# Loading the last rows of a convolution's input as f16 by GpSimd, in pieces of 5, 120 and 3 partitions

## The chip, the cores and the metric

The kernel runs on one core of a Trainium2 chip. The metric is the device time of one execution in microseconds (us). The kernel before takes 128.01 us (median; its first runs lay between 127.67 and 128.04). A profile accompanies the runs; its times count from the start of the profiled span, which is 1.8 us shorter than the device time. Sixteen DMA engines move all data between memory and the core. They are the subject of this document.

## The reference, cut to what matters

```python
batch, c_in, h, w, c_out, k, dilation = 16, 64, 64, 64, 128, 3, 2
x_pad = np.pad(x, ((0, 0), (0, 0), (pad, pad), (pad, pad)), mode='constant')
# for every image b, output channel co, input channel ci, and 3 x 3 taps kh, kw:
output[b, co] += weight[co, ci, kh, kw] * x_pad[b, ci, kh*dilation:kh*dilation+h, kw*dilation:kw*dilation+w]
```

Input is 16.8 MB and output 33.6 MB, both f32. That is what the DMA engines have to carry, whatever the arithmetic does.

## The kernel before: the parts that matter

Two images of 64 channels fill the 128 partitions; such a pair is loaded as f32, cast to f16 by ScalarE in four chunks of rows, multiplied by TensorE, summed by VectorE into an f32 output tile, and stored. There are eight pairs, and four groups of 16 output rows in each.

```python
    def load(pb, cuts=(0, H), queue=nc.sync):
        x32_tiles[pb] = fpool.tile([P, HW], f32, tag="x32", name="x32")
        for lo, hi in zip(cuts[:-1], cuts[1:]):
            queue.dma_start(
                out=x32_tiles[pb][:, lo * W : hi * W], in_=x_pair[pb, :, lo * W : hi * W]
            )
    # ... (cast(c) copies one chunk of rows, f32 to f16, on ScalarE)
    def casts(G):
        for n in range(2 if G else 3):
            c = ahead[0]
            if c >= ngroups or c > G + (7 if c < 2 * NG else 3):
                return
            cast(c)
            ahead[0] += 1
            if c % NG == NG - 1 and c // NG + XF < npairs:
                k = c // NG + XF
                load(k, (0, H) if k == XF else (0, H // 2, H), queue=nc.scalar)
    # ... (the loop over the 32 groups: products, copy of psP, two adds, then)
        if pb in (0, npairs - 1):
            if g % 2 == 1:
                store(pb, 0, (g - 1) * GR, (g + 1) * GR)
                store(pb, 1, (g - 1) * GR, (g + 1) * GR)
        elif g == NG - 1:
            store(pb, 0)
            store(pb, 1)
```

## Time and profile before

| | kernel before |
|---|---|
| time, median | 128.01 us |
| end of the last VectorE add | 109.9 us |
| end of the span | 126.2 us |
| last store: first, second last, last completion count | 121.46, 123.22, 125.23 us |

The view of windows gives, for stretches of the span, the busy time of each engine, TensorE's granted clock, the mean busy share of the 16 DMA engines and what they moved. The kernel before:

```profile
core 0: us, PE busy (x) PEld busy (x) DVE busy (x) ACT busy (x) POOL busy (x), PEclk, DMA share, GB/s
12.00:60.00 48.00, 47.56 (x462) 26.25 (x463) 42.54 (x47) 30.04 (x32) 0.00 (x0) 1.00 1.01 418
75.00:90.00 15.00, 15.00 (x148) 8.24 (x146) 13.18 (x15) 9.89 (x10) 0.00 (x0) 1.00 1.02 432
112.00:120.00 8.00, 0.00 (x0) 0.00 (x0) 0.00 (x0) 0.00 (x0) 0.00 (x0) 0.50 1.00 421
120.00:127.00 7.00, 0.00 (x0) 0.00 (x0) 0.00 (x0) 0.00 (x0) 0.00 (x0) 0.50 0.32 135
```

TensorE looks full until 108 us, but so do the DMA engines, and from 112 us on DMA works alone, at full rate. The SyncE queue's waits, in us in total, times, and longest, agree: the end of the kernel is a wait for stores.

```profile
SPq L279 <- DMA out_dram<-osb: 13.7, 1, 13.7
```

Two more lines of the page, the ScalarE casts and the DMA queues (packets, MB, share of the 16 engines' span):

```profile
L73 ACT CAST x<-x 128x1024 f16<-128x1024 f32 (+2 forms) x31 | 32.1, 1044 | 0.3 <-DMA x<-in_x_dram 0.3
...
q1 hardware_dynamic: 3600, 40.14, 75.5%
q10 hardware_dynamic: 1296, 10.49, 20.3%
```

One thing is not on the page. Each transfer has a semaphore which every DMA engine raises by one when its share has landed, and the trace records the time of each raise. For the last store of the kernel before, in us:

```
121.46 121.47 121.71 121.82 122.22 122.25 122.29 122.88 122.91 123.04 123.12 123.14 123.14 123.14 123.22 125.23
```

Fifteen engines finish within 1.8 us, and one comes 2.0 us after all others. I call these sixteen times the completion counts. The span ends 1.0 us after the last of them.

### The profile page before, as it was taken

How to read it: one execution, taken by the hardware profiler on the slowest of the kernel's cores; microseconds unless marked ns; L12 is line 12 of the kernel's file. 1: busy time of each engine (PE TensorE's matmuls, PEld its weight loads, DVE VectorE, ACT ScalarE, POOL GpSimd, SP SyncE). 2: the span in 40 equal slices, each digit the busy share in tenths (PEclk: the TensorE clock that was granted, in tenths of full speed). 3: DMA queues.
4: the chain of work that ended last, by engine and by line, in shares of the span. 5: the costliest groups of instructions: out<-in, count | busy, mean ns of one | idle time of the engine just before them, and what ended most of it. 6: DMA issues, size and time to landing. Idle time of an engine off the chain costs nothing.

```text
span 126.2 us, 2341 instructions
## 1 busy us (share of the span) xinstructions
PE 104.9 (83%) x1000; PEld 56.7 (45%) x1000; DVE 90.7 (72%) x103; ACT 65.0 (51%) x68; POOL 2.3 (2%) x8
## 2 busy tenths in 40 slices
PE   6984999999999999999999999999999999300000
PEld 2341555555555555555555555555556555100000
DVE  0650997988898888988979898889888887700000
ACT  4377794366656665666576666666666633000000
POOL 2400000000000000000000000000000000000000
PEclk9999999999999999999999999999999999955555
DMA  4999999899999999999999999999999999999960
GB/s 138 377 456 426 431 426 382 330 431 423 421 421 449 426 431 426 431 421 431 421 434 421 434 426 428 431 426 423 441 431 421 431 415 446 415 413 431 423 293 13
DMA packets 4906, 50.78 MB, mean 402 GB/s; under 512 B 544, under 2 KB 544, under 8 KB 800
## 3 DMA queue, kind: packets, MB, share of 16 engines
q1 hardware_dynamic: 3600, 40.14, 75.5%
q10 hardware_dynamic: 1296, 10.49, 20.3%
q8 instruction: 8, 0.13, 0.4%
q14 instruction: 2, 0.02, 0.0%
HBM read 17.07 MB, written 33.55 MB: 401 GB/s over the span
## 4 chain that ended last, share of the span: by engine, by line
PE 75%; DMA 6%; ACT 2%; issue 1%; DVE 1%; DVEq 1%; SPq 1%; ACTq 0%
PE psA L174 30%; PE psB L174 29%; PE psP L174 16%; DMA x<-in_x_dram 6%; DVE osb L233 1%; DVEq L279 1%; ACT p_sb L226 1%; ACT x L73 1%; SPq L64 0%; ACTq L64 0%; SPq L88 0%; DVEq L233 0%
## 5 line engine op out<-in xcount | busy, mean ns | idle before, releaser
L174 PEld LDWEIGHTS <-w_sb 64*128 64x128 f16 x960 | 54.6, 94 | 46.9 <-issue 2.1
L226 ACT COPY p_sb<-psP 128x1024 f32<-128x1024 f32 x32 | 32.4, 1012 | 37.5 <-PE psP L174 19.1
L233 DVE TENSOR_TENSOR osb<-psA,p_sb 128x1024 f32<-128x1024 f32 x32 | 39.2, 1224 | 14.3 <-PE psA L174 7.7
L174 PE MATMUL psA<-x,w_sb 64*128 64x496 f16 (+3 forms) x384 | 45.1, 365 | 0.5 <-ACT x L146 0.5
L174 PE MATMUL psB<-x,w_sb 64*128 64x496 f16 (+3 forms) x384 | 45.1, 365 | 0.0
L233 DVE TENSOR_TENSOR osb<-psB,p_sb 128x1024 f32<-128x1024 f32 x32 | 39.0, 1220 | 0.0
L73 ACT CAST x<-x 128x1024 f16<-128x1024 f32 (+2 forms) x31 | 32.1, 1044 | 0.3 <-DMA x<-in_x_dram 0.3
L174 PE MATMUL psP<-xs,w_sb 64*128 64x496 f16 (+1 forms) x192 | 26.0, 371 | 1.8 <-ACT p_sb L226 1.8
L85 DVE TENSOR_TENSOR xs<-x 128x512 f16<-128x512 f16 x32 | 13.3, 416 | 0.7 <-ACT x L73 0.7
L101 PE MATMUL dm<-zero 128*128 128x512 f16 x10 | 4.4, 561 | 1.2 <-DVE zero L93 1.2
L101 PEld LDWEIGHTS <-zero 128*128 128x128 f16 x10 | 1.1, 124 | 2.6 <-issue 1.3
L111 DVE CAST wd<-w 128x192 f16<-128x192 f32 x1 | 0.5, 505 | 2.4 <-DMA w<-in_weight_dram 2.4
L124 PEld LDWEIGHTS <-wd 128*64 128x64 f16 x30 | 1.0, 118 | 1.9 <-DVE wd L111 1.1
L124 PE MATMUL wt<-ident,wd 128*64 128x128 f16 x30 | 1.6, 241 | 0.2 <-DVE wd L111 0.2
L113 ACT ACT_TABLE_LOAD x1 | 1.3, 1283 | 0.7 <-PEq L265 0.7
L136 ACT CAST w_sb<-wt 128x384 f16<-128x384 f32 x1 | 0.5, 478 | 1.7 <-PE wt L124 1.7
L113 ACT CAST wd<-w 128x192 f16<-128x192 f32 x1 | 0.5, 538 | 1.5 <-DMA w<-in_weight_dram 1.5
L138 DVE CAST w_sb<-wt 128x384 f16<-128x384 f32 x1 | 0.6, 557 | 0.7 <-PE wt L124 0.7
L146 ACT CAST x<-x 128x512 f16<-128x512 f32 x1 | 0.6, 618 | 0.5 <-DMA x<-in_x_dram 0.5
L93 DVE MEMSET zero<- 128x256 uint32 x1 | 0.3, 272 | 0.9 <-PEq L265 0.9
L112 POOL TENSOR_TENSOR wd<-w 128x192 f16<-128x192 f32 x1 | 0.8, 807 | 2.3 <-DMA w<-in_weight_dram 2.3
L115 POOL CAST wd<-w 128x192 f16<-128x192 f32 x1 | 0.8, 803 | 0.0
(11 smaller groups left out, 3.8 us busy)
## 6 DMA issues: line engine op xcount, KB each, us to landing
out_dram<-osb SPq DMA_DIRECT2D x12, 2048.0 KB, 17.4
out_dram<-osb SPq DMA_DIRECT2D x8, 1024.0 KB, 14.6
x<-in_x_dram ACTq DMA_DIRECT2D x8, 1024.0 KB, 17.0
x<-in_x_dram SPq DMA_DIRECT2D x2, 2048.0 KB, 16.5
x<-in_x_dram ACTq DMA_DIRECT2D x1, 2048.0 KB, 15.3
x<-in_x_dram SPq DMA_DIRECT2D x1, 1088.0 KB, 5.6
x<-in_x_dram SPq DMA_DIRECT2D x1, 960.0 KB, 7.4
w<-in_weight_dram SPq DMA_DIRECT2D x1, 288.0 KB, 2.8
```

Source lines behind the costliest of these rows:

```text
L73: nc.scalar.copy(out=x16_tiles[pb][:, lo * W : hi * W], in_=x32_tiles[pb][:, lo * W : hi * W])
L85: nc.vector.tensor_tensor(out=s, in0=v[:, :, 0], in1=v[:, :, 1], op=add)
L101: nc.tensor.matmul(out=dm[:, 0:512], lhsT=zero[:, 0:P], rhs=zero)
L112: nc.gpsimd.tensor_tensor(out=wdv[:, 3], in0=wv[:, 0], in1=wv[:, 1], op=sub)
L113: nc.scalar.copy(out=wdv[:, 2], in_=wv[:, 0])
L115: nc.gpsimd.tensor_copy(out=wdv[:, 4], in_=wv[:, 2])
L124: nc.tensor.matmul(out=wts[k % 3][r * CI : (r + 1) * CI, c0 + j * CO : c0 + (j + 1) * CO], lhsT=wd[:, t * CI : (t + 1) * CI], rhs=ident,)
L138: nc.vector.tensor_copy(out=t2[0], in_=t2[1])
L174: nc.tensor.matmul(out=po, lhsT=w_sb[pp, t * CO : (t + 1) * CO], rhs=rhs, start=first and j == 1, stop=last and j == 2,)
L226: nc.scalar.copy(out=p_sb, in_=psP)
L233: nc.vector.tensor_tensor(out=o[:, :, b0 : b0 + NBLK, e], in0=ps.rearrange("p (m b q) -> p m b q", m=2, q=2 * W), in1=pv, op=add,)
L279: with _tile.TileContext(nc) as tc:
```

## The change

For the last pair, rows 34 to 63 are no longer loaded as f32 and cast. GpSimd's DMA queue, which can convert during the transfer, writes them as f16 into the tile that the products read. The 128 partitions go in pieces of 5, 120 and 3. A fourth, tiny load into `turned` is read by nobody.

```diff
+    def load_cast(pb, r0):
+        lo = 0
+        for n in (5, 120, 3):
+            nc.gpsimd.dma_start(
+                out=x16_tiles[pb][lo : lo + n, r0 * W :], in_=x_pair[pb, lo : lo + n, r0 * W :]
+            )
+            lo += n
+        nc.gpsimd.dma_start(out=turned[0:9], in_=x_pair[pb, 0:9, 0:16])
@@ cast
         if g == 0:
             x16_tiles[pb] = xpool.tile([P, HW], f16, tag="x16", name="x16")
+            if pb == npairs - 1:
+                load_cast(pb, 2 * GR + d)
@@ casts
-            cast(c)
+            if c < ngroups - 2:
+                cast(c)
             ahead[0] += 1
             if c % NG == NG - 1 and c // NG + XF < npairs:
                 k = c // NG + XF
-                load(k, (0, H) if k == XF else (0, H // 2, H), queue=nc.scalar)
+                cuts = (0, H // 2, H) if k > XF else (0, H)
+                load(k, cuts if k < npairs - 1 else (0, GR, 2 * GR + d), queue=nc.scalar)
```

The odd pieces only make sense as an attempt to spare one DMA engine. If a round-robin cursor (a pointer that remembers which engine comes next) hands one engine to each row of a small piece and fifteen engines to the 120 rows, then 5 + 15 + 3 + 9 is 32, two full turns of 16, and the tiny load is there to bring the cursor back to its start.

More of the change, by code (lines that the diff above doesn't have):

```diff
@@ L66, in load @@
             )
+    turned = wpool.tile([P, 16], f16, name="turned")
+    def load_cast(pb, r0):
[6 more added lines that the diff above has]
+        nc.gpsimd.dma_start(out=turned[0:9], in_=x_pair[pb, 0:9, 0:16])
     def cast(c):
```

## The prediction

> **What bounds the kernel.** Transfers. In the view of windows, 12 to 100 us has PE 87.6 of 88 us busy, but also DMA share 1.01 at 423 GB/s; after 108 us the engines are done (last matmul about 108.8, last VectorE add 109.9) while DMA runs on at 416 to 426 GB/s until about 120. SyncE's waits end with 13.7 us for the last stores. So the end is set by bytes: 50.78 MB over 16 DMA engines. And not evenly: in the trace's semaphore record, the last store's sixteen completion counts come at 121.46 to 123.22 us, and the last one at 125.23. One DMA engine is 2.0 us behind the next and 2.3 behind the median. The six stores before it show the same 2.0 us. That engine alone sets the end; the span closes 1.0 us after it.
>
> **What the change does.** It removes two casts of ScalarE (1.05 and 0.94 us) and adds four GpSimd issues. ScalarE is busy 51% and is not on the path: its relief is worth 0. The source bytes are the same (128 rows of 7,680 B, 291 ns per packet before); only the SBUF side halves, 0.49 MB.
> What counts is which engine carries which row. Before, each engine carried 8 rows of that piece. The Trainium skill ("DMA: Bandwidth & Descriptors", "Why a DMA increments its semaphore by 16 and not by 1") says that a transfer uses the largest k up to 16 that divides its partitions, and that a GpSimd transfer with k under 16 takes k consecutive engines from a round-robin cursor. So 5 rows go to five engines, 120 rows to the next fifteen (8 each), 3 rows to three starting at the engine left out; the tiny fourth load moves the cursor 9 more, 32 in all, back to its start. One engine then carries 2 rows instead of 8, six carry 9, nine carry 8. No trace shows this yet.
>
> **Cost.** If the light engine is the late one, it saves 6 x 291 ns = 1.75 us: its last count falls from 125.23 to about 123.5. The others may rise by one row, 123.22 + 0.29 = 123.5: balanced. Gain about 1.7 us, time about 126.3. If a cast packet costs by its f16 side (half, an estimate), the late engine saves 2.0 us. If the light engine is another, there is nothing to gain (0 to +0.3). I take the rotation of the cursor as aimed at the late engine, at 3 in 4.
>
> **Side effects.** The transfers wait for the third buffer of f16 x (pair 4's last product, about 73 us) and are needed at the row sum near 103: 30 us of room. They lie inside a saturated stretch, so total DMA work is conserved.
>
> **Prediction:** 126.4 us (-1.3%), range 125.6 to 128.1. Faster by over 2%: 0.07; within 2%: 0.90; slower: 0.03.
>
> **What would show it.** The last store's last count comes within 0.5 us of the second last, where it was 2.0; the second last stays within 0.4 us of 123.2; packets of the new queue take about 290 ns; PE still ends near 108.8; ScalarE busy falls by 2.0 us.
>
> **What would make it wrong.** The light engine is not the late one (gap stays 2.0, or grows by 0.3); cast packets run well over 291 ns; the late engine's delay comes back after 80 us; GpSimd's transfers add set-up at the start or end.

## The result, and the profile after

The changed kernel takes 128.49 us (median of four, 128.35 to 128.52). The ratio to the kernel before is 1.0041, with a 95% interval of 1.0023 to 1.0059. All ratios here are the mean time of one kernel's fast runs over that of the other's of the same rounds, so they are not quite the ratio of the medians that are quoted. The change made the kernel no faster (a loss of 0.4%), and the time is outside the predicted range by 0.4 us.

The same views after the change: windows, the wait at the end, the ScalarE casts, the queues, and GpSimd's issues (start, duration).

```profile
12.00:60.00 48.00, 46.89 (x454) 25.53 (x452) 41.16 (x46) 30.48 (x31) 0.00 (x0) 1.00 1.01 412
75.00:90.00 15.00, 15.00 (x148) 8.18 (x146) 13.29 (x15) 9.30 (x11) 0.56 (x2) 1.00 1.02 386
112.00:120.00 8.00, 0.00 (x0) 0.00 (x0) 0.00 (x0) 0.00 (x0) 0.00 (x0) 0.56 0.99 420
120.00:127.00 7.00, 0.00 (x0) 0.00 (x0) 0.00 (x0) 0.00 (x0) 0.00 (x0) 0.50 0.47 200
```

```profile
SPq L294 <- DMA out_dram<-osb: 12.5, 1, 12.5
```

```profile
L86 ACT CAST x<-x 128x1024 f16<-128x1024 f32 (+2 forms) x29 | 30.1, 1048 | 0.4 <-DMA x<-in_x_dram 0.4
...
q1 hardware_dynamic: 3600, 40.14, 75.9%
q10 hardware_dynamic: 1296, 9.50, 18.7%
q0 software_dynamic: 240, 0.49, 2.0%
```

```profile
73.34 1.72 POOL L73 DMA_DIRECT2D x<-in_x_dram  x3 [67.99 <-DVE osb L248]
75.04 0.52 POOL L77 DMA_DIRECT2D turned<-in_x_dram  x1
```

The casts fell by two and 2.0 us of ScalarE, and GpSimd issued its four transfers at 73.3 us, both as predicted. In the window from 75 to 90 us the rate seems lower, 386 instead of 432 GB/s. Of these 46 GB/s, 33 are bookkeeping: the record counts the 0.49 MB written as f16, no longer the 0.98 MB read (0.49 MB over 15 us). The wait at the end is 1.2 us shorter, but it began 1.3 us later.

The last store's completion counts after the change:

```
121.65 122.28 122.73 122.98 123.10 123.56 123.60 123.70 123.95 124.06 124.28 124.54 124.90 124.97 125.22 125.29
```

This looked to me like a success of the prediction, cancelled by something else: the gap of the last count is 0.07 us instead of 2.0, but all the others had come later; their mean rose from 122.69 to 123.80 us, with the last included. So the first theory, A or B below, was that the spared engine was the right one and that a common loss of 1.1 us ate the gain. Two things pointed to an early cause. TensorE's full clock is first recorded at 10.5 us in this profile and at 5.1 us in that of before. And by 70 us, before GpSimd did anything, the engines had moved 0.34 MB less (28.09 against 28.43 MB, summed from the packets), because some store packets between 41 and 61 us took up to 1.26 us instead of 0.61.

The clock shows in the timeline of one dummy matmul, first before, then after (start, duration in us):

```profile
5.79 0.39 PE L101 MATMUL dm<-zero 128*128 128x512 f16 x1
```

```profile
6.52 0.61 PE L114 MATMUL dm<-zero 128*128 128x512 f16 x1
```

### The profile page after: what moved, and what is told of

Read it like the earlier page. It is cut to its first block, busy times and chain, and to the rows that moved or that the text cites. A ratio compares the mean times of both kernels' runs of the same rounds, so it can differ in the third digit from the quotient of the medians.

```text
span 126.6 us, 2348 instructions
## 1 busy us (share of the span) xinstructions
PE 107.2 (85%) x1000; PEld 56.9 (45%) x1000; DVE 90.5 (72%) x103; ACT 63.2 (50%) x66; POOL 4.5 (4%) x12
## 4 chain that ended last, share of the span: by engine, by line
PE 82%; DMA 2%; DVE 1%; DVEq 1%; ACT 1%; issue 0%
PE psA L189 32%; PE psB L189 30%; PE psP L189 16%; DMA w<-in_weight_dram 2%; PE wt L137 2%; PE dm L114 2%; DVE osb L248 1%; DVEq L294 1%; ACT p_sb L241 1%; DVE wd L124 0%; DVEq L248 0%
## 5 line engine op out<-in xcount | busy, mean ns | idle before, releaser
L189 PE MATMUL psA<-x,w_sb 64*128 64x496 f16 (+3 forms) x384 | 46.1, 371 | 0.0
L86 ACT CAST x<-x 128x1024 f16<-128x1024 f32 (+2 forms) x29 | 30.1, 1048 | 0.4 <-DMA x<-in_x_dram 0.4
L114 PE MATMUL dm<-zero 128*128 128x512 f16 x10 | 5.0, 623 | 1.2 <-DVE zero L106 1.2
L73 POOL DMA_DIRECT2D x<-in_x_dram x3 | 1.7, 578 | 68.0 <-DVE osb L248 68.0
L137 PEld LDWEIGHTS <-wd 128*64 128x64 f16 x30 | 1.5, 162 | 2.6 <-DVE wd L124 1.3
L137 PE MATMUL wt<-ident,wd 128*64 128x128 f16 x30 | 2.2, 314 | 0.4 <-DVE wd L124 0.4
```

The costliest lines, as they stand in the source:

```text
L73: nc.gpsimd.dma_start(out=x16_tiles[pb][lo : lo + n, r0 * W :], in_=x_pair[pb, lo : lo + n, r0 * W :])
L86: nc.scalar.copy(out=x16_tiles[pb][:, lo * W : hi * W], in_=x32_tiles[pb][:, lo * W : hi * W])
L114: nc.tensor.matmul(out=dm[:, 0:512], lhsT=zero[:, 0:P], rhs=zero)
L137: nc.tensor.matmul(out=wts[k % 3][r * CI : (r + 1) * CI, c0 + j * CO : c0 + (j + 1) * CO], lhsT=wd[:, t * CI : (t + 1) * CI], rhs=ident,)
L189: nc.tensor.matmul(out=po, lhsT=w_sb[pp, t * CO : (t + 1) * CO], rhs=rhs, start=first and j == 1, stop=last and j == 2,)
```

## The experiments

Each kernel ran beside the kernel before on the same chip. There were eighteen runs after the first; e8 repeats the changed kernel, and e17 repeats e1. All gave correct results. The medians are of all executions of a run, the ratios of its fast ones alone (one execution of e4 and one of e17 were slow).

| run | GpSimd's pieces | median us | ratio (95%) |
|---|---|---|---|
| changed kernel | 5, 120, 3, tiny 9 | 128.49 | 1.0041 (1.0023 to 1.0059) |
| e8_after_again | the same | 128.49 | 1.0032 (0.9980 to 1.0085) |
| e1_even | 128 | 127.80 | 0.9977 (0.9949 to 1.0006) |
| e17_even_again | 128 | 128.38 | 1.0032 (1.0011 to 1.0052) |
| e7_four_even | 4 x 32 | 128.08 | 0.9978 (0.9933 to 1.0024) |
| e2_rot8 | tiny 8, 5, 120, 3, tiny 9, tiny 8 | 128.39 | 1.0035 (0.9991 to 1.0078) |
| e3_after_warm | 5, 120, 3, tiny 9 | 128.93 | 1.0063 (1.0024 to 1.0101) |
| e4_before_warm | none | 127.99 | 0.9991 (0.9963 to 1.0018) |
| e9_first4 | 4, 120, 4, tiny 9 | 128.20 | 1.0020 (1.0003 to 1.0037) |
| e10_first3 | 3, 120, 5, tiny 9 | 128.41 | 1.0037 (1.0015 to 1.0060) |
| e11_first2 | 2, 120, 6, tiny 9 | 128.34 | 1.0025 (1.0009 to 1.0042) |
| e18_120_8 | 120, 8 | 128.40 | 1.0046 (1.0029 to 1.0064) |
| e13_low4 | 96, 8 x 4 | 127.81 | 0.9982 (0.9948 to 1.0015) |
| e16_low5 | 88, 8 x 5 | 129.27 | 1.0092 (1.0056 to 1.0128) |

The five runs with tagged engines (e5, e6, e12, e14, e15) had one execution each and are told below.

### First call: is it the f16 path, the early clock, or the choice of the engine?

**e1_even**, one transfer over all partitions:

```diff
-        for n in (5, 120, 3):
-            nc.gpsimd.dma_start(... lo : lo + n ...)
-        nc.gpsimd.dma_start(out=turned[0:9], ...)
+        nc.gpsimd.dma_start(out=x16_tiles[pb][:, r0 * W :], in_=x_pair[pb, :, r0 * W :])
```

> The same f16 load by GpSimd, but in one transfer over all 128 partitions, so that nothing is moved between the DMA engines. Theory A (the redistribution works, and took the late engine back by about 1.5 us; a loss that is common to all engines cancels it, from the f16 path through GpSimd): the last engine stays about 2 us or more behind the second last, the median count of the last store stays near 123.8, and the time is 129.5 to 130.5 us. Theory B (the common loss is not of the f16 path but of this execution's early part, the late clock or collisions of stores): median count near 122.9, last engine about 2 us later, time 127.7 to 128.3. Theory C (the redistribution itself did nothing or harm): time at or below the changed kernel's 128.5, with the gap closed all the same.

**e2_rot8**, a tiny load of 8 rows ahead, and one of 8 behind:

```diff
+        nc.gpsimd.dma_start(out=turned2[0:8], in_=x_pair[pb, 0:8, 0:16])
         lo = 0
         for n in (5, 120, 3):
 ...
+        nc.gpsimd.dma_start(out=turned3[0:8], in_=x_pair[pb, 0:8, 0:16])
```

> The changed kernel with one tiny load of 8 rows ahead of the three pieces (and 8 more rows after, so that the cursor comes back): the engine that is spared is the one 8 places further. Theory A: the late engine is a fixed one and is not spared now, so the gap of the last store's last count is 2.0 to 2.6 us instead of 0.07, and the time is 1.3 to 2 us over the changed kernel, 129.8 to 130.5 us. Rival (no fixed late engine; the gap closed by chance or by the interleaving): gap under 1 us and time within 0.4 us of 128.5.

**e3_after_warm** and **e4_before_warm**, the changed kernel and the kernel before with one dummy matmul more:

```diff
-    dummies(6)
+    dummies(7)
```

> The changed kernel with seven instead of six dummy matmuls ahead of the weights, so that TensorE has no idle gap there. In the changed kernel's trace the full clock came at 10.5 us, in the kernel before at 5.1 us, and every store was issued 1.27 us later. Theory B (that delay shifts the stores against the loads and costs the common 1.1 us): full clock near 5 us, median count of the last store near 122.7 to 122.9, time 126.6 to 127.3. Theory A (the f16 path costs it): the clock may come early, the stores are issued 1 us earlier, the time stays 128.2 to 128.7.

> The kernel before with the same seventh dummy. Theory B: it had the early clock already in its profile, so within 0.3 us of the kernel before (127.7 to 128.2), and its spread over the rounds no larger. Theory A: the same. If it is over 0.5 us faster, the early clock is itself a matter of chance in the kernel before too.

The single f16 transfer took 127.80 us, so theory A's 129.5 fell. Its profiled execution was the slowest of its five (129.01 us; the others 127.70 to 127.97), so I do not read that profile for the time. The clock came at 6.6 us in the profile of e3_after_warm and its time was no better, 128.93 us: theory B's gain in time did not come. What B said of the counts does fit the traces. Full clock came after 10 us in two profiles only, the first of the changed kernel (10.5) and that of e1_even (10.2), and their last stores have median counts of 123.82 and 123.56 us. In the seventeen other profiles that are not slow it came by 6.6 us, and the median is 122.77 to 123.19, in that of e3_after_warm 122.97, where the last count was still 125.79. So the common lateness goes with the late clock and not with the pieces, though two profiles are an observation and no test, and without it the late engine is late again. Of e4_before_warm the profiled run was a slow one; its fast runs equal the kernel before. The Trainium skill ("TensorE: Matmul & The Clock Gate", "Part 1: The HAM clock gate (the "warmup" mystery)") says that the window that decides when the full clock comes runs freely and that the moment differs from run to run of the same kernel. The traces here agree: 10.5 us in the first profile of the changed kernel, 5.7 us in its second.

The rotation by 8 places changed nothing in the time, 128.39 us. Its profile had the late engine back, 1.80 us behind the second last (125.49 against 123.69). I took that as nearly what theory A expected of the gap (2.0 to 2.6), but the time it expected, 129.8, did not come.

### Second call: which engine is late?

Names for engines come from a trick. Four tiny loads of 4, 5, 8 and 12 rows follow the last store on the same queue. By the Trainium skill ("DMA: Bandwidth & Descriptors", "Why a DMA increments its semaphore by 16 and not by 1"), a transfer issued by SyncE uses the largest number of engines up to 16 that divides its rows, and takes the lowest-numbered ones. Each tiny load then waits its turn behind the store on exactly those engines. What the runs themselves show is the nesting: the load of 5 has the counts of the load of 4, each 0.17 to 0.19 us later, and one more.

```diff
+    for k in (4, 5, 8, 12):
+        nc.sync.dma_start(out=tags[k][0:k], in_=x_pair[0, 0:k, 0:16])
```

> The kernel before with four tiny loads of 4, 5, 8 and 12 rows behind its last store on the same queue. They move next to no bytes; each takes its place behind the store in the queues of the DMA engines that it uses, so its completion counts say when those engines finish. If such a load takes the lowest-numbered engines, the load of 5 holds one count more than the load of 4, that of engine 4, and the brackets 0 to 3, 4, 5 to 7, 8 to 11 and 12 to 15 can be told apart. Theory D (the spared engine is not the late one, which is a fixed one): the late count, some 2 us behind the others, is in no bracket or not in that of engine 4. The prediction's premise (the late engine is the one that the cursor spares, number 4 if the cursor starts at 0): the late count is in the loads of 5, 8 and 12 and not in that of 4. Theory E (no fixed late engine): another bracket than in the next run.

> The same four tiny loads behind the changed kernel. Theory D: the late count is in the same bracket as in the kernel before, and the spared engine, 1.7 us earlier than it would be, is the earliest count; if the cursor starts at 0 that earliest count is in the load of 5 and not in that of 4. Theory E: the late count is in another bracket than before.

**e7_four_even**: `for n in (32, 32, 32, 32)` and no tiny load.

> The f16 load by GpSimd in four transfers of 32 rows, 2 rows for every engine in each: four transfers, no redistribution. Theory D (the changed kernel pays for the ninth row on the late engine, 0.30 us, and not for the number of transfers): within 0.2 us of the single f16 transfer, about 127.8, and 0.4 to 0.7 us under the changed kernel of the same call. Rival F (what costs is that four transfers are set up, with sixteen completion counts each): within 0.2 us of the changed kernel.

**e8_after_again**: no edit.

> The changed kernel once more, on the same chip as the run of four even transfers. Theory D: 128.3 to 128.8, its profile with a last count 1.5 to 2.8 us behind the mean and a first count 1 us or more ahead of the mean. The prediction's reading of the first profile after (the late engine was taken back, the gap is 0.07 us): the gap stays under 0.5 us in this execution too.

The counts of the loads in e5_tag_before, where the last store ended at 123.95 and then 125.21 us:

```
load of 4: 121.72 121.82 122.17 122.39
load of 5: 121.89 122.00 122.34 122.58 125.39
```

The late count is in the load of 5 and not in that of 4: engine 4 is the late one in the kernel before. The prediction's aim at engine 4 was right. In e6_tag_after:

```
load of 4: 122.40 122.48 122.76 122.78
load of 5: 122.58 122.66 122.94 122.96 125.61
```

Engine 4 is as late after the change as before. It was not the one that was spared. (A second engine, between 8 and 11, was nearly as late in that execution.) The last store's first count, 120.57 us, is 1.1 us ahead of the next, so some engine was spared. I misread which: I took the 121.92 us that opens the load of 8 for that engine, and the load of 8 begins after engine 4, so I concluded 5, 6 or 7. But each tiny load comes after the store, and by a fraction of a microsecond: 120.57 has no partner in any of the four loads. The spared engine lies above 11.

The changed kernel again, e8_after_again, took 128.49 us. Its counts are what a second profile is for:

```
120.75 122.27 122.32 122.39 122.46 122.64 122.67 122.98 123.12 123.14 123.16 123.18 123.26 123.64 123.72 125.14
```

The late engine is 1.42 us behind the second last, and the spared one 1.5 us ahead of the second. The closed gap of the first profile was an accident of that execution, in which the other engines had been delayed.

Of the four even transfers, e7_four_even, theory D expected 0.4 to 0.7 us less than the changed kernel of the same call, and rival F about the same. The medians are 0.41 us apart (128.08 and 128.49), but the intervals overlap widely, so the times of this call decide nothing.

### Third call: move the spared engine

`for n in (5, 120, 3)` became (4, 120, 4), (3, 120, 5) and (2, 120, 6); e12_tag_after2 is the changed kernel with tiny loads of 5, 6, 7 and 16 rows.

> The changed kernel with pieces of 4, 120 and 4 rows: the spared engine moves one place down. The last runs showed that engine 4 is the late one, before and after the change, and that the spared engine of 5, 120, 3 is number 5, 6 or 7. Theory G (the mechanism of the prediction is right, only the cursor does not start at 0 but at 1, 2 or 3): one of the three kernels with 4, 3 and 2 rows in the first piece spares engine 4; its last store's last count falls from about 125.4 to about 123.6, no count is then over 1 us behind the second last, and its time is 126.6 to 127.2 us; the other two stay at 128.2 to 128.6. This one is it if the cursor starts at 1. Rival H (the late engine is fed by something that grows when it has room, or the rest of the kernel is the limit then): none of the three is under 127.5 us.

> Pieces of 3, 120 and 5 rows: the spared engine moves two places down. Theory G: this one spares engine 4 if the cursor starts at 2, then 126.6 to 127.2 us and a gap under 1 us; otherwise 128.2 to 128.6 us and a gap of about 2 us. Rival H: not under 127.5 us in any case.

> Pieces of 2, 120 and 6 rows: the spared engine moves three places down. Theory G: this one spares engine 4 if the cursor starts at 3, then 126.6 to 127.2 us and a gap under 1 us; otherwise 128.2 to 128.6 us and a gap of about 2 us. Rival H: not under 127.5 us in any case.

> The changed kernel with tiny loads of 5, 6, 7 and 16 rows behind its last store, to tell which of the engines 5, 6 and 7 is spared. Theory G: the earliest count, 1 us or more ahead of the next, is in the load of 6 and not in that of 5 if it is engine 5 (then the kernel with 4 rows first is the fast one), in that of 7 and not that of 6 if engine 6 (then 3 rows first), in neither if engine 7 (then 2 rows first). If the spared engine is not the same as there, the cursor's start differs between executions or chips.

None was fast: 128.20, 128.41 and 128.34 us, each with an early count near 120.4 to 121.0 and a late one 1.5 us behind the second last. In e12_tag_after2 the earliest count, 120.50, has its partner only in the load of 16 (120.67). If a cursor that starts at 1, 2 or 3 chose the engines, one of these kernels would have spared engine 4. None did: theory G, as it was put, fell. Which engine was spared in the three was not asked, so they do not rule out a cursor that starts elsewhere; the fourth call does.

What replaced it began from a line of the first profile after the change. Queue q0 of the changed kernel has 240 packets: 128 rows, 9 rows of the tiny load, and 103 packets of 4 bytes. Sixteen completion counts for each of four transfers make 64. The other 39 fit if every transfer is filled up to the same number of packets on all 16 engines: 16 - 5 = 11, 8 x 16 - 120 = 8, 16 - 3 = 13 and 16 - 9 = 7. The other kernels' q0 lines fit as well (e1_even, e7_four_even, e2_rot8, in this order):

```profile
q0 software_dynamic: 144, 0.49, 1.9%
```

```profile
q0 software_dynamic: 192, 0.49, 1.9%
```

```profile
q0 software_dynamic: 304, 0.49, 2.0%
```

Those are 128 + 16; 128 + 4 x 16; and 128 + 9 + 8 + 8 rows with 6 x 16 counts and 39 + 16 fillers. These lines show the filling, but not at which engine a transfer starts: a cursor would give the same counts for these pieces. Theory I adds that: every GpSimd transfer of n rows is laid out over all 16 engines from engine 0 upward, n/16 rows each, rounded up. The 120 rows give 8 to engines 0 to 14 and none to engine 15. The 5 and 3 rows add to the lowest engines. By it the change gave engine 15 none, engines 0 to 2 ten rows, 3 and 4 nine, and the late engine 4 one row more than before.

### Fourth call: the dose on engine 4

```diff
-        for n in (5, 120, 3):
+        for n in (96,) + 8 * (4,):    # e13_low4 (no tiny load)
+        for n in (88,) + 8 * (5,):    # e16_low5 (no tiny load)
```

e14_low4_tag is e13_low4 with tiny loads of 4, 5, 8 and 16 rows; e15_tag_after3 the changed kernel with tiny loads of 13, 14, 15 and 16.

> The f16 load in one piece of 96 rows and eight pieces of 4 rows. Theory I (no cursor: every GpSimd transfer of n rows starts at engine 0 and gives each engine n/16 rows, rounded up, in order, so 120 rows leave out engine 15 and nothing else, and 5 and 3 rows add to engines 0 to 4): engines 0 to 3 carry 6 + 8 = 14 rows, engine 4 and all above 6 instead of 8. The late engine 4 gains 2 x 304 ns = 0.6 us, less some 0.1 us for nine transfers; engines 0 to 3 finish near 124 and stay behind it. Last count about 124.7, time 127.4 to 127.8, against 128.0 for the kernel before. Theory G (a cursor that moves by 4 with each piece of 4): the eight pieces spread evenly, 8 rows each, time as the four even transfers, 127.9 to 128.2.

> The f16 load in one piece of 88 rows and eight pieces of 5 rows. Theory I: engine 4 belongs to the five that each small piece uses and carries 6 + 8 = 14 rows, 6 more than in an even load, 1.82 us: last count near 127, time 129.4 to 130.2 us, 2 us or more above the kernel with pieces of 4. Theory G (cursor): 40 rows over 16 engines, 2 or 3 each, beside 8 from the large piece at most: within 0.5 us of the kernel with pieces of 4.

> The kernel with pieces of 4 rows, with tiny loads of 4, 5, 8 and 16 rows behind its last store. Theory I: the load of 4 holds four counts near 123.5 to 124.3, later than in the kernel before (121.7 to 122.4); the load of 5 adds that of engine 4, still the last of all, at 124.7 to 125.2 instead of 125.4 to 125.6. Theory G: the four counts stay at 121.7 to 122.8.

> The changed kernel with tiny loads of 13, 14, 15 and 16 rows behind its last store. Theory I: the earliest count, 1 us or more ahead of the next, is in the load of 16 alone, so it is engine 15. Theory G: it is in the load of 13, 14 or 15 too.

In e15_tag_after3 the earliest count of the last store is 120.36 us. The loads of 15 and of 16 begin:

```
load of 15: 122.36 122.67 122.83
load of 16: 120.53 122.53 122.88
```

The early engine is in the load of 16 alone: the change spared engine 15.

By theory I the two kernels differ in this: with pieces of 5 and 88 rows, engine 4 carries 14 rows instead of 6, and engines 14 and 15 carry 4 and none instead of 6 each. The other engines carry the same. They took 127.81 and 129.27 us on the same chip: 1.46 us apart. A cursor would have given every engine 8 rows in the first, and none over 11 in the second (88 rows on eleven engines, 8 each, and the small pieces 2 or 3), so at 0.304 us a row an estimate of 0.9 us apart at most. In e14_low4_tag engines 0 to 3 had become late instead (123.70, 123.82, 124.04 and 125.04 us in the load of 4, against 121.72 to 122.39 in the kernel before, on another chip), and the count that the load of 5 adds, engine 4, is 124.89 us, down from 125.39. That all four lowest engines became late by 1.9 us and more is what eight pieces starting at engine 0 do; a cursor would have spread them. (I had expected engine 4 to be still the last of all; one of engines 0 to 3 was, at 125.04.) The filler rule fits too, 128 + 9 x 16 counts + 96 fillers in both (8 x 12 with pieces of 4; 8 + 8 x 11 with pieces of 5). Here it does decide something: 88 rows on eleven engines of 8 rows would have to be filled up by 40 and not by 8. The q0 lines of e13_low4 and of e16_low5:

```profile
q0 software_dynamic: 368, 0.49, 2.0%
```

```profile
q0 software_dynamic: 368, 0.49, 2.0%
```

As many packets, the same bytes, other engines, 1.46 us. The sizes were off: I had expected 129.4 us or more and a difference of 2 us or more. Between 6 and 14 rows the time moved by 0.18 us a row (1.46 us over 8), not by the packet's 0.30, and engine 4's own count in the traces by as little (124.70 in the last store of e14_low4_tag; 126.12, the last count, in e16_low5: 1.42 us). Its lateness is not simply the sum of its packets, and why not stays open.

### Fifth call: what does the 0.4 us consist of?

e17_even_again is e1_even once more; e18_120_8 has pieces of 120 and 8.

> The single f16 transfer over 128 partitions again, on the same chip as the next run. Theory I: engine 4 carries 8 rows as in the kernel before, so within 0.3 us of the kernel before, 127.7 to 128.1; the f16 path itself costs nothing that shows.

> Pieces of 120 and 8 rows and nothing else: engines 0 to 7 carry 9 rows, 8 to 14 carry 8, engine 15 none. Theory I: engine 4 has one row more than in the single transfer, 0.30 us, and one more transfer: 128.1 to 128.4 us, 0.3 to 0.5 us over the single transfer, its first count 1 us or more ahead of the second (engine 15) and its last count again about 2 us behind. Rival F (the loss of the changed kernel is that of four transfers and the small one): within 0.1 us of the single transfer.

The times did not settle it. The single transfer took 128.38 us here and 127.80 in the first call, on another chip; its two intervals do not overlap, so they do not cover what differs between calls. The pieces of 120 and 8 took 128.40, not apart from the single transfer of the same call. The spared engine was there once more (first count 120.09, second 121.88).

## Why the prediction was wrong

- **What bounds the kernel: right.** DMA runs at 421 GB/s from 112 to 120 us with all other engines done, and the last count of the last store sets the end. In e16_low5 and e13_low4 as many packets on other engines moved the time by 1.46 us.
- **ScalarE's relief is worth nothing: right.** 2.0 us less of casts, no gain.
- **Cast packets cost what f32 packets cost: right.** They took 304 ns, against 291 before. The half cost that the prediction held possible did not show.
- **The late engine is one fixed engine and the change is aimed at it: half right.** It is engine 4 in the runs that named it, and 5 + 120 + 3 + 9 fits a rotation that would spare engine 4 with a cursor that starts at 0.
- **"a GpSimd transfer with k under 16 takes k consecutive engines from a round-robin cursor": this step failed.** From it came "One engine then carries 2 rows instead of 8, six carry 9, nine carry 8". The runs showed that each piece starts at engine 0 (eight pieces of 4 rows made engines 0 to 3 late, 123.70 to 125.04 us against 121.72 to 122.39) and that the engine spared by 5, 120 and 3 is engine 15 (its count 120.36 us is in the load of 16 alone), so that 120 rows go to engines 0 to 14. By this rule engine 15 carried none of the rows and engine 4 nine. The gain of 1.7 us was not reduced or cancelled. It never existed. I should have seen the doubt: the same section of the skill says, in the paragraph that has the rule, that on trn2 some of GpSimd's direct copies use 16 engines with partitions/16 rows each, rounded up, and gives 100 and 127 rows as examples. I quoted the rule and left out the exception that turned out to hold for every piece here.
- **The chance that the wrong engine is spared: 1 in 4 was too little.** For that case the prediction said "0 to +0.3". Measured were ratios of 1.0041 and 1.0032, 0.48 and 0.38 us in the medians. A part of that is the set-up "at the start or end" that the prediction named among its risks without a number (next point).
- **What the 0.4 us consist of is settled in part.** From the last completion count to the end of the span it takes 1.01 us in the profile of the kernel before, 1.11 in those with one GpSimd transfer, 1.20 with two, and 1.26 to 1.29 with four or more (runs without tags). In that time SyncE checks the transfers' semaphores in pairs, one check every 0.06 us: three are left after the last count before the change and seven after it, because the four new transfers have semaphores of their own. That is some 0.27 us of the loss, which the readings above overlook; it is what rival F named, transfers and not rows. The ninth row on engine 4 is an estimate of 0.18 us, from the dose above. The runs with nine rows and with eight in the third call point the same way (128.41 and 128.34 against 128.20), but their intervals overlap. What is left is within what one and the same kernel differs by between calls (1.0032 against 0.9977 for the single transfer).
- **The check in the prediction was not enough.** "within 0.5 us of the second last, where it was 2.0" came true in the first profile after, 0.07 us, for a wrong reason. The second half of that check, "the second last stays within 0.4 us of 123.2", failed at once (125.22), and that should have been read as: not the late engine came earlier, the others came later.

No version that ran beat both kernels clearly. e13_low4 is under the changed kernel (127.81 against 128.49, on another chip), but from the kernel before it is not apart (0.9982, interval 0.9948 to 1.0015). If all pieces start at engine 0, none can spare engine 4 alone; pieces of 4 can only heap rows on engines 0 to 3, which then become late themselves. What makes engine 4 late was found only in part. The packet record of the kernel before has no engine numbers, but an engine's packets run back to back and can be followed. Followed back from the late count, with eight packets between two counts at every step, nineteen 16 KB packets of stores between 95 and 107.5 us took 633 to 653 ns, where nearly all of the other engines' took 611. Eight such packets a store are 0.3 us, and by about that much the gap grows from store to store, 0.95, 1.22, 1.50, 1.81 and 2.02 us between 90 and 111 us. The last of these slow packets starts at 108.2 us; TensorE's last matmul ends at 108.6; from 110 us on the packets take as long as the others' and the gap stays at 2.0. Why that engine's packets are slower while TensorE works stays open. It was not tested, since nothing in the program addresses that engine.

## What to carry to other kernels

When a kernel ends in stores, look at the completion counts of the last transfer, engine by engine: a mean DMA share of 1.0 hides an engine that is 2 us late. Before moving work away from an engine, name the engine in a run, by tiny loads behind the last transfer, and check by the same loads where the new transfers really went. Count what follows the last transfer, too: here each new transfer's semaphore cost up to 0.1 us at the end. And take a second profile before you believe that a gap closed: one execution's sixteen times can look right by accident.

## What the Trainium skill lacked or had wrong

- "DMA: Bandwidth & Descriptors", "Why a DMA increments its semaphore by 16 and not by 1": for GpSimd's copies it gives the cursor as the rule and the layout over 16 engines, rounded up, as an exception for "some direct copies", without saying which. Here all that ran fits the exception, with every transfer starting at engine 0. Three sizes decide it: eight pieces of 4 rows made engines 0 to 3 late (123.70 to 125.04 us against 121.72 to 122.39), 88 rows were filled up by 8 packets and not by 40, and after pieces of 5, 120 and 3 the early count, 120.36 us, was engine 15's.
- The same section does not say that such a transfer is filled up to equal packets on all engines. The counts show 39 packets of 4 bytes beyond the completion counts for 5, 120, 3 and 9 rows, 96 for 88 and 8 x 5.
- "DMA: Bandwidth & Descriptors", "Latency and other measured facts" names engines 7 and 15 as usually slower, with GpSimd's descriptor rings as a guess. In the tagged run of the kernel before, which issues no GpSimd transfer, engine 4 was late by 1.3 us to the second last, and no other by as much. Since the page ties 7 and 15 to GpSimd's path, this is an addition and no contradiction.
- No page gives the cost of a packet that is cast from f32 to f16: 7,680 bytes read and 3,840 written took 304 ns at the median, and the f32 packet of the same row 291 ns.
